# Sixteen experts in a row: gathers over the first seven, scatters from the eighth on

## The chip, the cores and the metric

One Trainium2 chip, one of its cores. The time is device microseconds of one launch. The kernel before takes 2141.14 us (median of three runs, 2135.18 to 2143.14); the execution that was profiled took 2138.47 us.

## The reference, cut to what matters

One layer of a diffusion backbone over 512 latent tokens of 1024 channels. A token mixer comes first; the change lies wholly in the mixture of experts behind it. Each of 16 experts takes the 64 tokens that have the highest affinity for it, and all matrices are fp32:

```python
def ec_moe(h, router, w1, w3, w2):
    b_, n, _ = h.shape
    cap = EC_CAPACITY * n // N_EXPERTS          # 64
    aff = jax.nn.softmax(jnp.einsum('bld,de->ble', h, router).astype(F32), axis=-1)
    gate, idx = lax.top_k(jnp.swapaxes(aff, 1, 2), cap)
    xe = h[bidx, idx]
    hid = jax.nn.silu(jnp.einsum('becd,edf->becf', xe, w1)) * jnp.einsum('becd,edf->becf', xe, w3)
    ye = jnp.einsum('becf,efd->becd', hid, w2) * gate[..., None].astype(h.dtype)
    return jnp.zeros_like(h).at[bidx, idx].add(ye)
```

w1, w3 and w2 of an expert are 1024 x 1024 each, 12 MiB together; all 192 MiB are read once.

## The kernel before, in words

**Experts.** `experts` (L1678) runs over e = 0 to 15. An expert has four parts on TensorE. `front` (L1701) makes the two input products, `ph`, from its 64 gathered tokens `xe` and the eight pieces of w1 and w3; a piece is 1 MiB. In the **gap** behind it ScalarE copies `ph` out, `hidden` (L1769) transposes it (`pht`) and ScalarE and VectorE make silu times the second product, in two halves. `gates` (L1781) makes the gate of each slot (`pgt`), from experts 4 to 14 also `by_slot` (L1762), the transposed one-hot rows by slot (`poh`, kept in `O[e]`). `back` (L1791) makes the output product `pye` from four pieces of w2, a `yield` after each, and scales it into `yf[e]`. `split` (L1809) cuts `yf[e]` into a high and a low part, `Y[e]`.

**Gathers and scatters.** `gather(h)` (L1657) makes `xe` for experts 4h to 4h+3 as products of the tokens (`xH`, `xL`) with one-hot matrices `OH`; it has eight units, each 8 matmuls `rp` and one ScalarE copy. `scatter` (L1817) adds the results of a pair of experts to the 512 rows of `acc` (`psc` on TensorE, `macc` on VectorE), in eight units. `acc` and `ys` (which holds `O` and `Y`) lie in the memory of `xH` and `xL`, so no scatter can come before the last gather. Where the loop hands a generator to `front` as `fill`, its units stand between the input products; where it hands it to `more`, they stand in the gap: two ahead of each half of `hidden` and the rest behind (`GB`, L54).

**What sets the order.** Inside the experts TensorE's order is the order of the code (`ME`, L64); the other engines' is set by a scheduler. The number of gather units in the gap of expert e is `GU[e]` (L53). The 24 units of gathers 1 to 3 stand at experts 1, 2 and 3; scatters of pairs (0,1), (2,3), (4,5) in the gaps of experts 4, 5, 6; those of (6,7) to (12,13) as `fill` in the fronts of experts 8, 10, 12 and 14.

**The weight stream.** SyncE issues the weight pieces in order (`w_load`, L1587). Eighteen are asked for before the stage; from then on 13 buffers (`slots`) go round, so a piece is issued when TensorE has used the piece that its buffer held.

Of the kernel before, what the change touches and what calls it, by code (L numbers as in the profile page):

```python
# [8 lines left out]
F32 = mybir.dt.float32  # L9
# [9 lines left out]
D = 1024  # L19
# [30 lines left out]
WA = 8  # L50
SP = 1
CP = 0
GU = 0, 6, 9, 9  # L53
GB = 2, 2, 2  # L54
WC = 0
WB = 50
# [30 lines left out]
class Block:  # L87
# [1569 lines left out]
    def gather(self, ps, tags, h):  # L1657

        nc = self.nc
        xH, xL = self.xHL  # L1660
        if h < 3:
            x = (self.rp if h == 2 else self.op).tile([128, 1 + h // 2, KT, 4, 64], F32, name="xe", tag="B" if h == 2 else f"xe{h}")
            self.xe += [x[:, j] for j in range(1 + h // 2)]
        oh = self.op.tile([128, 4, 4, 64], F32R, name="OH", tag="OH", bufs=1)
        n = 4 if h else 1
        for i in range(0, 4, n):
            self.one_hot(oh[:, i:i + n], self.posT[:, i:i + n, 4 * h:4 * h + 4])
        for kt in range(KT):
            pt = ps.tile([128, 256], F32, name="rp", tag=tags[kt % len(tags)], bufs=2)
            for i in range(4):  # L1670
                o = oh[:, i].rearrange("p e s -> p (e s)")
                nc.tensor.matmul(pt, xH[:, i, kt * 128:kt * 128 + 128], o, start=i == 0, stop=False)
                nc.tensor.matmul(pt, xL[:, i, kt * 128:kt * 128 + 128], o, start=False, stop=i == 3)
            nc.scalar.activation(self.xe[h][:, kt].rearrange("p e s -> p (e s)"), pt, AF.Identity,
                                 bias=self.mod2[:, 1, kt:kt + 1], scale=self.mod2[:, 0, kt:kt + 1])
            yield

    def experts(self, slots, hl, rp, pool, ps):  # L1678
# [76 lines left out]
        def twice(e):  # L1755

            if e not in OH:
                o2 = OH[e] = self.op.tile([128, 4, 2, 64], F32R, name="o2", tag="o2", bufs=1)
                self.one_hot(o2, self.posT[:, :, e:e + 1].to_broadcast([128, 4, 2]))
            return OH.pop(e).rearrange("p i a s -> p i (a s)")  # L1760

        def by_slot(e, o2):  # L1762
            po = ps.tile([128, 512], F32, name="poh", tag="pt", bufs=2)
            for i in range(4):
                nc.tensor.transpose(po[:, i * 128:i * 128 + 128], o2[:, i].bitcast(F32), self.ident)
            O[e] = self.ys[:, 4 + e % 4]
            nc.scalar.activation(O[e], po, AF.Copy)
# [13 lines left out]
        def gates(e):  # L1781

            o2 = twice(e)
            pg = ps.tile([128, 2], F32, name="pgt", tag="pt", bufs=2)
            for i in range(4):
                nc.tensor.matmul(pg, o2[:, i], self.affr[:, i, e], start=i == 0, stop=i == 3)
            nc.vector.reduce_sum(self.gate[:, e:e + 1], pg, axis=AX.X)
            if 3 < e < 15:
                by_slot(e, o2)

        def back(e):  # L1791

            py = ps.tile([128, 512], F32, name="pye", tag="py", bufs=2)
            for k in range(4):
                w2 = take(12 * e + 8 + k)
                for j in range(2):
                    kt = 2 * k + j
                    for c in range(2):
                        nc.tensor.matmul(py[64 * c:64 * c + 64], hd[e][:, kt], w2[j][:, 512 * c:512 * c + 512],  # L1799
                                         start=kt == 0, stop=kt == 7, skip_group_check=True)  # L1800
                yield
            if e == 15:
                return py
            yf[e] = yfs.rearrange("p a (b f) -> p (a b) f", b=2)[:, e % 4]
            nc.scalar.activation(yf[e], py, AF.Copy, scale=self.gate[:, e:e + 1])
            if e > 6:
                split(e)

        def split(e):  # L1809

            Y[e] = [self.ys[:, 2 * (e % 2) + h] for h in range(2)]
            for h, y in enumerate(Y[e]):
                own, other = slice(64 * h, 64 * h + 64), slice(64 - 64 * h, 128 - 64 * h)
                nc.scalar.activation(y[own], yf[e][own], AF.Copy)  # L1814
                nc.vector.tensor_sub(y[other], yf[e][own], y[own].bitcast(F32))  # L1815

        def scatter(grp):  # L1817
            for i in range(4):
                for h in range(2):
                    pc = ps.tile([128, 512], F32, name="psc", tag="psc", bufs=2)  # L1820
                    for k, e in enumerate(grp):
                        nc.tensor.matmul(pc, O[e][:, i * 128:i * 128 + 128], Y[e][h], start=k == 0, stop=k == len(grp) - 1)  # L1822
                    a = self.acc[:, i, 512 * h:512 * h + 512]
                    if grp[0] == 0:
                        nc.vector.tensor_copy(a, pc)
                    else:
                        nc.vector.tensor_add(a, a, pc)  # L1827
                    yield
# [50 lines left out]
                nc.sync.dma_start(self.out[0, i * 128:i * 128 + 128, :], self.acc[:, i])  # L1879
        if SP:  # L1880
            self.tc.keep_in_program_order(nc.scalar.activation(self.gate[:, 0:1], self.eps, AF.Sigmoid))
        rest = itertools.chain(*(self.gather(ps, ["psc"], h) for h in (1, 2, 3)))
        for e in range(16):
            g, fill, steps = iter(()), iter(()), 8 * (1,)

            more = itertools.islice(rest, GU[e]) if e < 4 else iter(())
            if e == 0:
                g = self.gather(ps, ["pt", "psc"], 0)
                next(g)
            elif e in (4, 5, 6):  # L1890
                if e == 6:
                    split(5)
                more = scatter([2 * e - 8, 2 * e - 7])
            elif 7 < e < 15 and e % 2 == 0:
                fill = scatter([e - 2, e - 1])
            elif e == 13:

                fin = self.op.tile([128, 4, 512], F32, name="fin", tag="xe0")
                fin2 = self.op.tile([128, 4, 512], F32, name="fin", tag="xe1")
                idx = fin2[:, 1, 176:177].bitcast(I32)  # L1900
                G = fin2[:, 2:4].rearrange("p a f -> p (a f)")
                nc.gpsimd.dma_start(G, self.Gd[1:2, :].to_broadcast([128, D]))
                Gh, pairs, row, half = fin[:, 0], fin2[:, 1, 0:128], fin2[:, 1, 128:132], fin2[:, 1, 132:133]
                for h in range(2):
                    nc.gpsimd.dma_start(Gh[64 * h:64 * h + 64], self.Gd[1:2, 512 * h:512 * h + 512].to_broadcast([64, 512]))
                for h in range(2):
                    nc.vector.tensor_add(pairs[:, 64 * h:64 * h + 64], self.ident[:, 0:64], self.ident[:, 64:128])
                nc.gpsimd.iota(row, pattern=[[256, 4]], base=0, channel_multiplier=2, allow_small_or_imprecise_dtypes=True)
                nc.vector.memset(half, 0.0)
                nc.vector.memset(half[64:128], 1.0)  # L1910
                nc.gpsimd.tensor_scalar(G, G, -.5, None, op0=OP.mult)
                nc.gpsimd.tensor_scalar(Gh, Gh, -.5, None, op0=OP.mult)
                o2 = twice(15)
                fill = itertools.chain(places(o2), tokens(fin[:, 1], self.x1, o2))
            elif e == 15:
                o2 = twice(15)
                OH[15] = o2.rearrange("p i (a s) -> p i a s", a=2)
                sc, tk = scatter([14]), tokens(fin[:, 2], self.acc, o2)
                fill = (next(sc if x == "s" else tk, None) for x in FO)
                with self.tc.manual_schedule(engines=set(ML)):  # L1920
                    py = front_last(fill, ST)
                break
            front(e, g, fill, steps)
            for f in range(3):
                for _ in range(GB[f]):
                    next(more, None)
                if f < 2:
                    hidden(e, f)
            self.finish(more)
            if e == 3:  # L1930
                self.finish(rest)
                self.acc = hl.tile([128, 4, D], F32, name="macc", tag="hlH")
                self.ys = hl.tile([128, 8, 512], F32R, name="yhl", tag="hlL")
            for n in {3: (0, 1), 4: (2, 3)}.get(e, ()):
                by_slot(n, twice(n))
            for n in {3: (0, 1), 4: (2, 3), 5: (4,), 7: (6,)}.get(e, ()):
                split(n)
            gates(e)
            self.finish(back(e))

        (x, a, y), g = (fin[:, i] for i in (1, 2, 3)), fin2[:, 0]
        ss, rs = fin2[:, 1, 133:134], fin2[:, 1, 134:135]
# [173 lines left out]
```

## Time and profile before

| | |
|---|---|
| median of three runs | 2141.14 us |
| profiled execution | 2138.47 us |
| span of its trace | 2136.7 us |
| TensorE busy | 1880.0 us (88%) |
| VectorE busy | 1244.5 us (58%) |
| ScalarE busy | 840.0 us (39%) |
| mean granted TensorE clock | 0.933 |

The page also cuts the span into 40 slices of 53.4 us. TensorE's digits are 9 through the experts' stage up to its end (slices 31 to 39), and a busy digit does not tell products that pace the kernel from products that could have come earlier. The line under it, gigabytes a second, stands at 292, 355, 333 and 362 in slices 31 to 34 and at 409 in slices 35 to 39. Read the two together: where the bytes run at one steady top rate, the stream sets the pace; where they fall below it, something holds the stream back.

### The profile page before, as it was taken

To read this page: it belongs to the slowest core of one execution; us is meant where nothing else is said; L and a number is where in the kernel's file an instruction comes from. 1 tells how busy PE (TensorE), PEld (TensorE's weight loads), DVE (VectorE), ACT (ScalarE), POOL (GpSimd) and SP (SyncE) were. 2 spreads that over 40 slices of the span, in tenths; PEclk is the share of its full clock that TensorE was granted. 3 is DMA by queue.
4 is the path that set the end of the run, shared out by engine and by line. 5 is a ranking of instruction groups with operands and counts; after the bars stand their busy time and mean duration, and the time that the engine had idled before them with its cause. 6 is when DMAs were issued, how large, how long until landed. Compare 5 with 4: busy or idle time off the path is not lost.

```text
span 2136.7 us, 34532 instructions
## 1 busy us (share of the span) xinstructions
PE 1880.0 (88%) x13683; PEld 1255.7 (59%) x13696; DVE 1244.5 (58%) x2234; ACT 840.0 (39%) x1344; POOL 259.2 (12%) x383
## 2 busy tenths in 40 slices
PE   5978898888869988999998997799999999999997
PEld 2867676676646756667675664377877453433332
DVE  4466988897888567555654898864364022322224
ACT  5454565545624343443543453353233131111113
POOL 1123323133220000000000000000001000000002
PEclk8999989999979989999998998889999999999998
DMA  6357687777888766785536353358567989999997
GB/s 239 89 128 179 161 201 181 177 175 184 206 199 241 229 225 217 257 254 157 180 102 203 121 170 104 108 180 287 187 247 292 355 333 362 409 409 409 409 409 292
DMA packets 388414, 495.13 MB, mean 232 GB/s; under 512 B 138521, under 2 KB 278031, under 8 KB 385179
## 3 DMA queue, kind: packets, MB, share of 16 engines
q1 hardware_dynamic: 349883, 407.33, 57.4%
q0 software_dynamic: 21504, 68.70, 11.0%
q10 hardware_dynamic: 16864, 16.88, 2.5%
q8 instruction: 108, 1.77, 0.3%
q14 instruction: 55, 0.45, 0.1%
HBM read 393.96 MB, written 97.98 MB: 230 GB/s over the span
## 4 chain that ended last, share of the span: by engine, by line
PE 53%; DVE 18%; DMA 13%; ACT 8%; issue 6%; POOL 1%; SPq 1%; ACTq 0%; POOLq 0%; DVEq 0%
PE ph L1712 9%; PE pl L311 9%; DMA wraw<-in_w_in_dram 5%; PE pye L1799 5%; PE pch L901 4%; PE mp L1361 4%; PE pc L314 3%; DVE wlo L286 2%; DMA ew<-in_exp_w_dram 2%; PE psc L1822 1%; PE sps L1180 1%; ACT whi L283 1%; PE py L901 1%; PE pl L1314 1%; PE adaps L167 1%
## 5 line engine op out<-in xcount | busy, mean ns | idle before, releaser
L311 PE MATMUL pl<-hlH,whi 128*128 128x512 f32 x672 | 244.1, 443 | 14.2 <-ACT u L455 5.6
L311 PE MATMUL pl<-hlH,wlo 128*128 128x512 f32 x672 | 236.3, 428 | 0.0
L311 PE MATMUL pl<-hlL,whi 128*128 128x512 f32 x672 | 231.9, 425 | 0.0
L1713 PE MATMUL ph<-ew,xe 128*64 128x512 f32 x432 | 196.3, 597 | 2.1 <-DMA ew<-in_exp_w_dram 2.1
L1712 PE MATMUL ph<-ew,xe 128*64 128x512 f32 x432 | 196.0, 596 | 0.0
L283 ACT ACTIVATE whi<-wraw 128x1024 fp32r<-128x1024 f32 x93 | 97.8, 1052 | 182.2 <-DMA wraw<-in_w_in_dram 79.1
L311 PEld LDWEIGHTS pl<-hlH,whi 128*128 128x128 f32 x672 | 132.8, 202 | 56.7 <-issue 14.1
L286 DVE TENSOR_TENSOR wlo<-wraw,whi 128x1024 fp32r<-128x1024 f32 x93 | 112.8, 1212 | 84.1 <-ACT whi L283 58.7
L311 PEld LDWEIGHTS pl<-hlL,whi 128*128 128x128 f32 x672 | 129.3, 196 | 38.1 <-issue 11.4
L311 PEld LDWEIGHTS pl<-hlH,wlo 128*128 128x128 f32 x672 | 128.3, 196 | 36.6 <-issue 12.6
L1712 PEld LDWEIGHTS ph<-ew,xe 128*64 128x64 f32 x432 | 56.3, 137 | 105.9 <-issue 104.5
L1799 PE MATMUL pye<-ew,ewx 128*64 128x512 f32 x448 | 108.3, 635 | 0.0
L314 PE MATMUL pc<-hcH,whi 128*128 128x256 f32 (+1 forms) x312 | 97.2, 315 | 7.1 <-ACT u L455 6.1
L464 DVE SCALAR_TENSOR_TENSOR cacc<-u,cst,cacc 128x772 f32<-128x772 f32 (+1 forms) x96 | 93.3, 972 | 11.1 <-ACT cacc L460 9.6
L314 PE MATMUL pc<-hcL,whi 128*128 128x256 f32 (+1 forms) x312 | 94.6, 307 | 0.0
L314 PE MATMUL pc<-hcH,wlo 128*128 128x256 f32 (+1 forms) x312 | 94.4, 304 | 0.0
L1719 ACT ACTIVATE ewx<-ph 128x512 f32<-128x512 f32 x30 | 17.9, 598 | 187.2 <-PE ph L1713 170.0
L1827 DVE TENSOR_TENSOR macc<-macc,psc 128x512 f32<-128x512 f32 x56 | 37.7, 685 | 91.4 <-PE psc L1822 91.3
L314 PEld LDWEIGHTS pc<-hcH,whi 128*128 128x128 f32 (+1 forms) x312 | 63.0, 202 | 15.8 <-ACT u L455 9.2
L1799 PEld LDWEIGHTS pye<-ew,ewx 128*64 128x64 f32 x448 | 32.7, 146 | 63.8 <-issue 63.1
L1815 DVE TENSOR_TENSOR yhl<-yf,yhl 64x512 fp32r<-64x512 f32 x30 | 20.5, 686 | 81.0 <-ACT yhl L1814 80.5
L1217 ACT ACTIVATE X<-selb,ncumT 128x128 f32<-128x128 f32 x128 | 36.4, 367 | 78.4 <-PE selb L1214 78.3
(594 smaller groups left out, 4100.4 us busy)
## 6 DMA issues: line engine op xcount, KB each, us to landing
ew<-in_exp_w_dram SPq DMA_DIRECT2D x126, 1024.0 KB
ew<-in_exp_w_dram SPq DMA_DIRECT2D x90, 512.0 KB
wraw<-in_w_in_dram SPq DMA_DIRECT2D x83, 512.0 KB
adaw<-in_ada_w_dram SPq DMA_DIRECT2D x24, 1024.0 KB
cst<-in_exp_w_dram SPq DMA_DIRECT2D x14, 1024.0 KB
BTd<-BT ACTq DMA_DIRECT2D x48, 256.0 KB
sAL<-ALd SPq DMA_DIRECT2D x23, 512.0 KB
sBT<-BTd SPq DMA_DIRECT2D x23, 512.0 KB
```

The lines of the kernel that those rows point to most:

```text
L283: pin(nc.scalar.activation(hi, raw, AF.Copy))
L286: self.lo.tensor_sub(lo, raw, hi.bitcast(F32))
L311: nc.tensor.matmul(pl[:n], w_[:, kt, :n], x[0][:, kt, :], **e)
L314: nc.tensor.matmul(pc[:n], w_[:, kt, :n], x[1][:, kt, :], **e)
L464: e.scalar_tensor_tensor(acc[:, s0:s0 + n0], u[:, s0 + k:s0 + k + n0], cw[:, b, k:k + 1], acc[:, s0:s0 + n0], op0=OP.mult, op1=OP.add)
L901: mm = lambda o, w, x, f=True, l=True: nc.tensor.matmul(o, w, x, start=f, stop=l, skip_group_check=True)
L1217: nc.scalar.activation(X[:, c], pt[d][:, c], AF.Identity, bias=self.ncumT[:, c, r:r + 1])
L1361: nc.tensor.matmul(po[ob], w[k][lo][:, ob * 128:ob * 128 + 128], yb[k][:, h], start=k + h + lo == 0, stop=k == 15 and lo == 1)
L1712: nc.tensor.matmul(ph[e][f][0:64], x, w1[j][:, fs], start=kt == 0, stop=kt == 7, skip_group_check=True)
L1713: nc.tensor.matmul(ph[e][f][64:128], x, w3[j][:, fs], start=kt == 0, stop=kt == 7, skip_group_check=True)
L1799: nc.tensor.matmul(py[64 * c:64 * c + 64], hd[e][:, kt], w2[j][:, 512 * c:512 * c + 512], start=kt == 0, stop=kt == 7, skip_group_check=True)
L1827: nc.vector.tensor_add(a, a, pc)
```

## The change: what it does

The gather units are spread: 3, 3, 2, 6, 5, 5 in the gaps of experts 1 to 6. `xe` of gather 2 takes the memory of gather 0, and gather 3 goes into a tile of the memory that held two early weight pieces and gathers 2 and 3 before. As `acc` and `ys` now come after expert 6, the outputs of experts 0 to 7 wait in `yf` (those of 4 to 7 in the other half of that tile). The seven pairs are scattered in the gaps of experts 7 to 12 and 14, none in a front. The rows by slot of experts 0 to 9 are made from a new one-hot during the output products of the expert ahead of the scatter: one after two pieces, one after all four.

On ScalarE, expert 2 of the kernel before, from its copies of `ph` (`ewx<-ph`) to its result (`yf`); `xe<-rp` is a gather unit, `ewx<-pht` a half of the activation:

```order
L1719 ACTIVATE ewx<-ph 128x512 x2
L1674 ACTIVATE xe<-rp,mod_7996 128x256 x2
L1777 ACTIVATE ewx<-pht 128x256
L1674 ACTIVATE xe<-rp,mod_7996 128x256 x2
L1777 ACTIVATE ewx<-pht 128x256
L1674 ACTIVATE xe<-rp,mod_7996 128x256 x5
L1805 ACTIVATE yf<-pye,gate 128x512
```

The same expert in the changed kernel:

```order
L1720 ACTIVATE ewx<-ph 128x512 x2
L1675 ACTIVATE xe<-rp,mod_7996 128x256 x2
L1778 ACTIVATE ewx<-pht 128x256
L1675 ACTIVATE xe<-rp,mod_7996 128x256
L1778 ACTIVATE ewx<-pht 128x256
L1806 ACTIVATE yf<-pye,gate 128x512
```

Nine units have become three; the five that followed the second half are gone.

On TensorE, the gap and output products of expert 8 of the kernel before, whose front holds a scatter (its last unit is the first row):

```order
L1822 MATMUL psc<-yhl 128x512 x2
L1775 MATMUL pht<-ident,ewx 128x128 x8
L1786 MATMUL pgt<-rt_14982,o_16454 128x2 x4
L1765 MATMUL poh<-ident,o_16454 128x128 x4
L1799 MATMUL pye<-ew,ewx 64x512 x16
```

The same stretch of the changed kernel:

```order
L1823 MATMUL psc<-yhl 128x512 x4
L1776 MATMUL pht<-ident,ewx 128x128 x4
L1823 MATMUL psc<-yhl 128x512 x4
L1776 MATMUL pht<-ident,ewx 128x128 x4
L1823 MATMUL psc<-yhl 128x512 x8
L1787 MATMUL pgt<-rt_14982,o_16351 128x2 x4
L1800 MATMUL pye<-ew,ewx 64x512 x8
L1766 MATMUL poh<-ident,o_16359 128x128 x4
L1800 MATMUL pye<-ew,ewx 64x512 x8
L1766 MATMUL poh<-ident,o_16384 128x128 x4
```

The whole scatter has moved into the gap, and two groups of rows by slot, of experts 4 and 5, cut the output products.

```diff
@@ -50,7 +50,7 @@
 WA = 8
 SP = 1
 CP = 0
-GU = 0, 6, 9, 9
+GU = 0, 3, 3, 2, 6, 5, 5
 GB = 2, 2, 2
 WC = 0
 WB = 50
@@ -1659,8 +1659,9 @@
         nc = self.nc
         xH, xL = self.xHL
         if h < 3:
-            x = (self.rp if h == 2 else self.op).tile([128, 1 + h // 2, KT, 4, 64], F32, name="xe", tag="B" if h == 2 else f"xe{h}")
-            self.xe += [x[:, j] for j in range(1 + h // 2)]
+            self.xe.append(self.op.tile([128, KT, 4, 64], F32, name="xe", tag=f"xe{h % 2}"))
+        else:
+            self.xe.append(self.later[:, 1].rearrange("p a (k e s) -> p (a k) e s", e=4, s=64))
         oh = self.op.tile([128, 4, 4, 64], F32R, name="OH", tag="OH", bufs=1)
         n = 4 if h else 1
         for i in range(0, 4, n):
@@ -1785,7 +1786,7 @@
             for i in range(4):
                 nc.tensor.matmul(pg, o2[:, i], self.affr[:, i, e], start=i == 0, stop=i == 3)
             nc.vector.reduce_sum(self.gate[:, e:e + 1], pg, axis=AX.X)
-            if 3 < e < 15:
+            if 9 < e < 15:
                 by_slot(e, o2)
 
         def back(e):
@@ -1801,9 +1802,9 @@
                 yield
             if e == 15:
                 return py
-            yf[e] = yfs.rearrange("p a (b f) -> p (a b) f", b=2)[:, e % 4]
+            yf[e] = (self.later[:, 0] if 3 < e < 8 else yfs).rearrange("p a (b f) -> p (a b) f", b=2)[:, e % 4]
             nc.scalar.activation(yf[e], py, AF.Copy, scale=self.gate[:, e:e + 1])
-            if e > 6:
+            if e == 14:
                 split(e)
 
         def split(e):
@@ -1879,21 +1880,20 @@
                 nc.sync.dma_start(self.out[0, i * 128:i * 128 + 128, :], self.acc[:, i])
         if SP:
             self.tc.keep_in_program_order(nc.scalar.activation(self.gate[:, 0:1], self.eps, AF.Sigmoid))
+        SC = {7: (0, 1), 8: (2, 3), 9: (4, 5), 10: (6, 7), 11: (8, 9), 12: (10, 11), 14: (12, 13)}
         rest = itertools.chain(*(self.gather(ps, ["psc"], h) for h in (1, 2, 3)))
         for e in range(16):
             g, fill, steps = iter(()), iter(()), 8 * (1,)
 
-            more = itertools.islice(rest, GU[e]) if e < 4 else iter(())
+            more = itertools.islice(rest, GU[e]) if e < 7 else iter(())
             if e == 0:
                 g = self.gather(ps, ["pt", "psc"], 0)
                 next(g)
-            elif e in (4, 5, 6):
-                if e == 6:
-                    split(5)
-                more = scatter([2 * e - 8, 2 * e - 7])
-            elif 7 < e < 15 and e % 2 == 0:
-                fill = scatter([e - 2, e - 1])
-            elif e == 13:
+            elif e == 4:
+                self.later = self.rp.tile([128, 2, 2, D], F32, name="ewB2", tag="B")
+            elif e in SC:
+                more = scatter(SC[e])
+            if e == 13:
 
                 fin = self.op.tile([128, 4, 512], F32, name="fin", tag="xe0")
                 fin2 = self.op.tile([128, 4, 512], F32, name="fin", tag="xe1")
@@ -1912,7 +1912,7 @@
                 nc.gpsimd.tensor_scalar(Gh, Gh, -.5, None, op0=OP.mult)
                 o2 = twice(15)
                 fill = itertools.chain(places(o2), tokens(fin[:, 1], self.x1, o2))
-            elif e == 15:
+            if e == 15:
                 o2 = twice(15)
                 OH[15] = o2.rearrange("p i (a s) -> p i a s", a=2)
                 sc, tk = scatter([14]), tokens(fin[:, 2], self.acc, o2)
@@ -1927,16 +1927,23 @@
                 if f < 2:
                     hidden(e, f)
             self.finish(more)
-            if e == 3:
+            if e == 6:
                 self.finish(rest)
                 self.acc = hl.tile([128, 4, D], F32, name="macc", tag="hlH")
                 self.ys = hl.tile([128, 8, 512], F32R, name="yhl", tag="hlL")
-            for n in {3: (0, 1), 4: (2, 3)}.get(e, ()):
-                by_slot(n, twice(n))
-            for n in {3: (0, 1), 4: (2, 3), 5: (4,), 7: (6,)}.get(e, ()):
-                split(n)
             gates(e)
-            self.finish(back(e))
+            outputs = back(e)
+            for n in SC.get(e + 1, ()):
+                if n < 10:
+                    o2 = twice(n)
+                    next(outputs)
+                    next(outputs)
+                    by_slot(n, o2)
+                if n < e:
+                    split(n)
+            self.finish(outputs)
+            if e in SC.get(e + 1, ()):
+                split(e)
 
         (x, a, y), g = (fin[:, i] for i in (1, 2, 3)), fin2[:, 0]
         ss, rs = fin2[:, 1, 133:134], fin2[:, 1, 134:135]
```

## Rows read from the trace of the kernel before

**Rows 1.** Windows of the experts' stage: length, busy time, granted clock, DMA share, GB/s
```profile
core 0: us, PE busy (x) PEld busy (x) DVE busy (x) ACT busy (x) POOL busy (x), PEclk, DMA share, GB/s
1640.00:1660.00 20.00, 19.18 (x106) 9.71 (x106) 2.81 (x6) 4.74 (x9) 0.00 (x0) 1.00 0.81 300
1660.00:1680.00 20.00, 20.00 (x96) 6.48 (x92) 0.67 (x2) 1.20 (x2) 0.00 (x0) 1.00 0.84 316
1680.00:1700.00 20.00, 20.00 (x122) 11.50 (x122) 2.44 (x6) 5.32 (x11) 0.00 (x0) 1.00 0.93 360
1700.00:1720.00 20.00, 19.03 (x126) 12.82 (x124) 3.43 (x7) 6.83 (x13) 0.00 (x0) 1.00 1.02 409
1720.00:1740.00 20.00, 20.00 (x94) 6.46 (x90) 0.14 (x1) 1.28 (x2) 0.00 (x0) 1.00 0.92 353
1740.00:1760.00 20.00, 15.93 (x104) 12.58 (x104) 7.89 (x13) 9.72 (x18) 2.60 (x3) 0.88 0.79 294
1760.00:1780.00 20.00, 20.00 (x89) 6.35 (x86) 0.00 (x0) 1.34 (x3) 0.00 (x0) 0.95 0.96 359
1780.00:1800.00 20.00, 15.90 (x66) 8.22 (x67) 11.28 (x20) 5.40 (x10) 0.00 (x0) 0.83 0.79 307
1800.00:2080.00 280.00, 268.17 (x1194) 100.34 (x1192) 67.21 (x127) 43.16 (x77) 3.52 (x3) 0.99 1.03 409
```
**Rows 2.** Timeline, TensorE: first product of experts 2, 3, 4 and 5
```profile
1694.21 0.59 PE L1712 MATMUL ph<-cst,xe 128*64 128x512 f32 x1
1726.20 0.59 PE L1712 MATMUL ph<-ew,xe 128*64 128x512 f32 x1
1765.91 0.59 PE L1712 MATMUL ph<-ew,xe 128*64 128x512 f32 x1
1801.52 0.59 PE L1712 MATMUL ph<-ew,xe 128*64 128x512 f32 x1
```
**Rows 3.** Timeline, TensorE: expert 5 from its gap to expert 6
```profile
1815.35 1.19 PE L1822 MATMUL psc<-yhl 128*128 128x512 f32 x4
1821.90 0.66 PE L1765 MATMUL poh<-ident,o 128*128 128x128 f32 x4
1822.48 7.09 PE L1799 MATMUL pye<-ew,ewx 128*64 128x512 f32 x32
1829.40 0.59 PE L1712 MATMUL ph<-ew,xe 128*64 128x512 f32 x1
```
**Rows 4.** Timeline, TensorE: gap of expert 1
```profile
1680.14 0.38 PE L1672 MATMUL rp<-OH,xH 128*128 128x256 f32 x1
1682.16 0.60 PE L1775 MATMUL pht<-ident,ewx 128*128 128x128 f32 x4
1686.86 0.50 PE L1786 MATMUL pgt<-rt,o 128*128 128x2 f32 x4
```
**Rows 5.** Timeline, SyncE: issues of weight pieces round expert 3's gap
```profile
1740.12 0.88 SPq L1595 DMA_DIRECT2D ew<-in_exp_w_dram  x2
1759.83 4.05 SPq L1595 DMA_DIRECT2D ew<-in_exp_w_dram  x4
```
**Rows 6.** Timeline, TensorE: waits in experts 2, 3, 4, and expert 3's output products
```profile
1711.63 0.36 PE L1672 MATMUL rp<-OH,xH 128*128 128x256 f32 x1 [0.97 <-DVE OH L1655]
1755.16 1.01 PE L1786 MATMUL pgt<-rt,o 128*128 128x2 f32 x4 [1.87 <-ACT yhl L1767]
1756.11 9.97 PE L1799 MATMUL pye<-ew,ewx 128*64 128x512 f32 x32
1789.16 1.07 PE L1765 MATMUL poh<-ident,o 128*128 128x128 f32 x4 [2.64 <-DVE o L1655]
```
**Rows 7.** One line's instructions: the one-hot rows, durations min/median/max
```profile
L1655 DVE TENSOR_TENSOR o<-rt x21: 679/692/694, 1633.5 to 2085.5; 128x512 fp32r<-128x512 f32 x21
```
**Rows 8.** Timeline, TensorE: its last wait for a weight piece
```profile
2061.54 0.64 PE L1713 MATMUL ph<-ew,xe 128*64 128x512 f32 x1 [0.34 <-DMA ew<-in_exp_w_dram]
```
**Rows 9.** Windows: where the weight stream ends
```profile
2116.00:2120.00 4.00, 4.00 (x21) 1.29 (x17) 3.93 (x5) 2.28 (x4) 4.00 (x4) 1.00 0.82 329
```

## The prediction, before the run

> **What bounds the kernel now.** I looked first at the page's row of gigabytes a second by slice, because the experts do one fixed thing: read 192 MiB once. From 1800 to 2080 us the windows show 409 GB/s with the DMA engines' share at 1.03 [rows 1]: no more fits. One piece of 1 MiB (1.0486 MB) then takes 1.0486/0.409 = 2.56 us, and an expert's twelve 30.8 us. That is the pace of the second half, whatever TensorE does.
>
> Next I asked what held the stream below 409 before 1800. The same windows give 300, 316, 360, 409, 353, 294, 359 and 307 from 1640 on [rows 1]. The starts of the experts on TensorE say why: expert 2 takes 1726.20 - 1694.21 = 32.0 us, expert 3 39.7, expert 4 35.6 [rows 2], all longer than 30.8, while expert 5 takes 1829.40 - 1801.52 = 27.9 [rows 2, 3]. The 13 buffers are full, and a piece can be asked for only when an old one has been used. SyncE's own rows show it: nothing is issued between 1740.12 and 1759.83 [rows 5], while TensorE stands in expert 3's gap and begins its output products at 1756.11 [rows 6]. So early on TensorE paces the stream, later the stream paces itself, and bytes not moved early can't be caught up later at a rate that is already full.
>
> The third view is the end. TensorE's last wait for a piece is at 2061.54 [rows 8], and the rate falls off in the window from 2116 [rows 9]; I take 2117 for the last piece. From 2061.54 on TensorE runs through its own work, a few us behind the stream.
>
> **The change part by part.** Prices first. The front without insertions takes 1815.35 - 1801.52 = 13.8 us [rows 2, 3]. From the front's end to the next expert it is 1829.40 - 1815.35 = 14.05 with a scatter in the gap [rows 3], and 1694.21 - 1680.14 = 14.07 with six gather units [rows 2, 4]: the two fillings cost the same, 27.9 us for the expert. Two gather units and the switch behind them take 1682.16 - 1680.14 = 2.0 us [rows 4], so I price a unit at 1.0. One group of rows by slot takes 1822.48 - 1821.90 = 0.6 us [rows 3].
>
> With these, TensorE's need in the changed kernel:
> - Experts 1 and 2, three units each: 27.9 - 3 x 1.0 = 24.9. Expert 3, two units: 23.9. Where a gap becomes short, a wait for the activation comes back, under 1 us of it.
> - Expert 4, six units: 27.9. Expert 5, five units, with the turn from gather 2 to 3 inside the gap: 26.9 plus the 0.97 that this turn cost in expert 2 [rows 6] = 27.9.
> - Expert 6, five units and two groups of rows: 26.9 + 1.2 = 28.1.
> - Experts 7 to 9, a scatter, two groups of other experts' rows, none of its own: 27.9 + 1.2 - 0.6 = 28.5. Expert 10, all three groups: 29.1. Experts 11, 12 and 14: 27.9, as expert 5.
> - Expert 13 keeps its fill.
>
> Every one is below the stream's 30.8. Experts 2 to 5 together need 24.9 + 23.9 + 27.9 + 27.9 = 104.6 us instead of 1829.40 - 1694.21 = 135.2. But those 30.6 us are not the gain: TensorE may go no further ahead than the pieces. The gain is what the stream had lost. Its shortfall against 409 from 1680 to 1800 is 49 + 0 + 56 + 115 + 50 + 102 = 372 GB/s, in windows of 20 us [rows 1]: 7.44 MB, or 18.2 us at 409. The shortfall of 1640 to 1680, 109 + 93 = 202, belongs to expert 0, which is unchanged, and to the first buffers; that stays. Of the 49 in 1680 to 1700, the gap of expert 1, I leave 20 standing, since a shorter gap is still a gap: 1.0 us. So the last piece lands 17.2 us sooner, about 2100.
>
> Does the end follow it? Before, TensorE ended its products behind the last piece, and expert 15 is unchanged. Expert 14 gets shorter on TensorE, but the last quarter of its front must still wait for its pieces, and gap, output products and expert 15 follow as one dense chain. So I take the same distance: end earlier by 17.2. What appears in its place are waits of TensorE for pieces, some 30.8 - 28.5 = 2.3 us an expert from about expert 6 on.
>
> What I cost at nothing. The gather and scatter instructions are the same in number. Six more one-hots are built, 0.69 us each on VectorE [rows 7], 4 us in all; the first stands behind the gate's reduction while TensorE has half of its output products to do (7.09/2 = 3.5 us [rows 3]), the second has the other half. If that cover fails, TensorE stands at the transposes; the price is in the second rival. The scatter leaves the fronts of experts 8, 10, 12 and 14; that frees TensorE, which then waits longer for pieces: nothing. Results of experts 4 to 7 go into the tile of two early pieces; those are used up in expert 1. SyncE's list of pieces is in the same order. On GpSimd two loads of the last scale now wait for expert 11's front and stand behind the other load; what is queued behind them is wanted only in expert 15.
>
> A rule of the Trainium skill speaks against the full sum. Its page "DMA: Bandwidth & Descriptors", section "Where 436 GB/s comes from", says that for HBM to SBUF the HBM side binds at about 358 GB/s per core. Counted against 358, only 353, 294 and 307 fall short, by 120 GB/s over 20 us, an estimate of 6.7 us of gain. The trace disagrees, with 409 over 280 us [rows 1], on a core that runs alone; the measurement decides.
>
> Sum: 2138.47 - 18.2 + 1.0 = 2121.3 us. The profiled execution lies 2.7 us below the median 2141.14. I forecast 2121, with 2115 to 2127 as its own range: the price of a gather unit hardly matters, since there are 2 to 6 us of room per expert, and what remains is how much of expert 1's loss returns, and the distance at the end.
>
> **The rivals.**
>
> The stream is freed wholly. If the pieces of experts 0 and 1 also came at 409, the shortfall of 1640 to 1800 would all return: 574 GB/s x 20 us / 409 = 28.1 us, 2110. For it: expert 1 uses its pieces sooner. Against: expert 0 is the same, and some of the first buffers are used once only. This is a floor, since TensorE's own 30.6 us and the shorter later fronts can't outrun the pieces.
>
> The rows by slot stall. In experts 3 and 4, where the kernel before built rows for other experts, TensorE stood 1.87 us for a ScalarE copy and 2.64 for a one-hot [rows 6]. If each of experts 6 to 10 pays both, 28.5 + 4.5 = 33.0 against 30.8, it loses 2.2 x 5 = 11 us: 2132. For: the same instructions on the same three engines, and the splits stand between. Against: the stalls came where two groups and the splits stood back to back; now 3.5 us of products lie between.
>
> The clock, the slow side. Waits are exactly what this change adds to TensorE. In expert 3, behind its waits, the output products took 9.97 us [rows 6] where 7.09 is the full price [rows 3], 2.9 more, and the granted clock of the window round their start is 0.88, of 1780 to 1800 0.83 [rows 1], a mixture of the levels 1.2 and 2.4 GHz. If each of experts 6 to 14 paid 2.9 twice, once behind a wait for pieces in the front and once behind the gap, it would need 28.5 + 5.8 = 34.3, 3.5 over the stream, 31 us in nine experts: 2138.5 - 17.2 + 31 = 2152. It decides from 28.5 + x > 30.8 + 17.2/9, that is x = 4.2 us lost per expert. The Trainium skill's "TensorE: Matmul & The Clock Gate", section "HAM oscillation — how this bites in real kernels", tells of this chain: a wait for DMA in every tile, and each next tile starts cold. Against: the trace's waits for pieces are short (0.34 us [rows 8]), a slow stretch only shortens the next wait, since the stream runs on, and from 1800 to 2080 the clock was 0.99 [rows 1] with gaps in every expert.
>
> The change doesn't free the stream. If the pauses of SyncE came from the queue itself, the rate would stay as it is: 2138. Against: the pause ends 3.7 us after the output products of expert 3 begin, when the first of their pieces is used [rows 5, 6].
>
> **How the numbers follow.** Forecast 0.70, stream wholly freed 0.09, stalls at the rows 0.09, clock 0.06, not freed 0.06. A difference under 0.5%, 10.7 us, can't be told from no change. Faster: 0.70 + 0.09 = 0.79. Same: stalls and not freed, 0.15. Slower: clock, 0.06. The range, 2110 to 2133, goes from the floor to the stalls and leaves out the last two, 0.12.
>
> **What would show it.** Right: 400 GB/s and more in every window from 1700 to the end; experts 1 to 3 at 24 to 26 us each on TensorE; waits of TensorE for `ew` in most experts from 6 or 7 on, 15 to 25 us in all; no pause of SyncE as long as the one at 1740; experts 7 to 14 at about 30.8 us. Wrong: windows under 380 between 1700 and 1800 (a gap still holds the stream); waits for one-hots or copies at the transposes of experts 6 to 10; a granted clock under 0.9 from expert 6 on with experts longer than 31 us; or the last piece at 2100 and the end no nearer to it.

## The result: 0.8% faster, by what the stream had lost

The changed kernel takes 2122.66 us (median of 5 runs, 2119.16 to 2128.71), the kernel before 2139.74 beside it (5 runs): ratio 0.9921, interval 0.9897 to 0.9946. The forecast was 2121, the range 2110 to 2133. The profiled execution took 2122.66 us, its span is 2120.9.

The instructions ahead of expert 0 are the same in both kernels, yet expert 0 began anywhere from 1635 to 1648 us in the profiled runs of this study. So I also measure the **stage**, from expert 0's first `ph` to the end of the last `pye`: two executions of the changed kernel, with starts 5 us apart, gave 471.71 and 471.60. First and last row of it on TensorE in the kernel before (start us, duration us):

```profile
1635.09 0.64 PE L1712 MATMUL ph<-ew,xe 128*64 128x512 f32 x1
...
2120.44 3.65 PE L1799 MATMUL pye<-ew,ewx 128*64 128x512 f32 x16
```

The changed kernel, with the starts of experts 2 to 6 on the way:

```profile
1636.56 0.64 PE L1713 MATMUL ph<-ew,xe 128*64 128x512 f32 x1
...
1693.14 0.59 PE L1713 MATMUL ph<-cst,xe 128*64 128x512 f32 x1
...
1718.51 0.59 PE L1713 MATMUL ph<-ew,xe 128*64 128x512 f32 x1
...
1744.13 0.59 PE L1713 MATMUL ph<-ew,xe 128*64 128x512 f32 x1
...
1772.03 0.59 PE L1713 MATMUL ph<-ew,xe 128*64 128x512 f32 x1
...
1800.17 0.59 PE L1713 MATMUL ph<-ew,xe 128*64 128x512 f32 x1
...
2104.62 3.65 PE L1800 MATMUL pye<-ew,ewx 128*64 128x512 f32 x16
```

The stage was 2124.09 - 1635.09 = 489.00 and is 2108.27 - 1636.56 = 471.71 us: 17.3 shorter. The span shows 15.8 of it, since expert 0 began 1.5 us later. Experts 2, 3 and 4 take 25.4, 25.6 and 27.9 us, where they took 32.0, 39.7 and 35.6 [rows 2].

The windows of the changed kernel, in the columns of [rows 1]:

```profile
1640.00:1660.00 20.00, 19.53 (x104) 9.18 (x100) 1.86 (x3) 4.60 (x9) 0.00 (x0) 1.00 0.82 305
1660.00:1680.00 20.00, 19.65 (x94) 7.04 (x96) 1.62 (x5) 1.07 (x2) 0.00 (x0) 1.00 0.81 309
1680.00:1700.00 20.00, 19.89 (x108) 9.22 (x106) 2.26 (x6) 4.13 (x8) 0.00 (x0) 1.00 1.02 406
1700.00:1720.00 20.00, 19.89 (x110) 9.37 (x108) 2.26 (x6) 4.13 (x8) 0.00 (x0) 1.00 1.03 410
...
1780.00:1800.00 20.00, 19.03 (x112) 10.28 (x110) 3.56 (x7) 4.58 (x9) 0.00 (x0) 1.00 1.03 409
1800.00:2064.00 264.00, 249.26 (x1146) 100.27 (x1142) 75.75 (x140) 50.21 (x91) 6.12 (x6) 1.00 1.03 408
...
2100.00:2104.00 4.00, 4.00 (x20) 1.19 (x16) 3.93 (x5) 2.26 (x3) 4.00 (x4) 1.00 0.81 327
```

Read the last column downward: from 1680 to 2064 us the stream stands at 406 to 410 GB/s, where it was 294 to 409 up to 1800; in the first two windows it is what it was. It falls off in the window from 2100, before in that from 2116 [rows 9]. SyncE, which paused from 1740.12 to 1759.83 [rows 5], now issues without such a pause. The 15 issues from 1725.57 on are 12 pieces, since three of the 13 buffers are filled in two halves; the last row ends where the view was cut:

```profile
1725.57 29.38 SPq L1595 DMA_DIRECT2D ew<-in_exp_w_dram  x15
1755.84 0.37 SPq L1595 DMA_DIRECT2D cst<-in_exp_w_dram  x1
1757.12 14.94 SPq L1595 DMA_DIRECT2D ew<-in_exp_w_dram  x7
```

What TensorE waits for in the changed kernel (us in all, times, longest): on its matmul rows from 1630 to 2121,

```profile
PE ph L1714 <- DMA ew<-in_exp_w_dram: 9.5, 13, 1.5
PE pgt L1787 <- DVE ewx L1780: 2.7, 3, 1.3
...
PE ph L1714 <- DMA cst<-in_exp_w_dram: 1.5, 1, 1.5
```

and on its weight loads, `PEld`, from 1800 to 2070 (the first column of numbers is again the sum):

```profile
PEld ph L1714 <- DMA ew<-in_exp_w_dram: 23.6, 18, 2.3
```

Both say that TensorE now waits for pieces. The sizes differ, since the matmul rows count idle time only from the modelled end of the products still in flight.

### The profile page after: what moved, and what is told of

The parts are those of the page before. It is cut to its first block, busy times and chain, and to the rows that moved or that the text cites. A ratio compares the mean times of both kernels' runs of the same rounds, so it can differ in the third digit from the quotient of the medians.

```text
span 2120.9 us, 34560 instructions
## 1 busy us (share of the span) xinstructions
PE 1865.1 (88%) x13683; PEld 1251.7 (59%) x13696; DVE 1245.5 (59%) x2240; ACT 838.0 (40%) x1344; POOL 256.3 (12%) x383
## 3 DMA queue, kind: packets, MB, share of 16 engines
q0 software_dynamic: 21504, 68.70, 11.1%
## 4 chain that ended last, share of the span: by engine, by line
PE 50%; DVE 18%; DMA 17%; ACT 7%; issue 6%; SPq 1%; POOL 1%; ACTq 0%; POOLq 0%; DVEq 0%
PE pl L311 9%; PE ph L1713 6%; DMA ew<-in_exp_w_dram 5%; DMA wraw<-in_w_in_dram 5%; PE pch L901 4%; PE pye L1800 4%; PE mp L1361 4%; PE pc L314 3%; DVE wlo L286 2%; PE pl L1314 2%; PE sps L1180 1%; PE py L901 1%; DMA BTd<-BT 1%; PE adaps L167 1%; PE ph L1714 1%
## 5 line engine op out<-in xcount | busy, mean ns | idle before, releaser
L1714 PE MATMUL ph<-ew,xe 128*64 128x512 f32 x336 | 148.8, 594 | 4.4 <-DMA ew<-in_exp_w_dram 4.4
L311 PEld LDWEIGHTS pl<-hlL,whi 128*128 128x128 f32 x672 | 128.5, 195 | 37.9 <-issue 11.4
L1713 PE MATMUL ph<-ew,xe 128*64 128x512 f32 x336 | 148.7, 594 | 0.0
L311 PEld LDWEIGHTS pl<-hlH,wlo 128*128 128x128 f32 x672 | 127.3, 195 | 35.6 <-issue 11.7
L1800 PE MATMUL pye<-ew,ewx 128*64 128x512 f32 x448 | 101.4, 597 | 0.0
L1713 PEld LDWEIGHTS ph<-ew,xe 128*64 128x64 f32 x336 | 44.7, 137 | 78.9 <-issue 76.5
L1779 DVE TENSOR_TENSOR ewx<-ewx,pht 128x256 f32<-128x256 f32 x32 | 13.4, 419 | 108.3 <-ACT ewx L1778 108.0
L314 PEld LDWEIGHTS pc<-hcL,whi 128*128 128x128 f32 (+1 forms) x312 | 60.7, 196 | 4.4 <-issue 2.1
```

The costliest lines, as they stand in the source:

```text
L311: nc.tensor.matmul(pl[:n], w_[:, kt, :n], x[0][:, kt, :], **e)
L314: nc.tensor.matmul(pc[:n], w_[:, kt, :n], x[1][:, kt, :], **e)
L1713: nc.tensor.matmul(ph[e][f][0:64], x, w1[j][:, fs], start=kt == 0, stop=kt == 7, skip_group_check=True)
L1714: nc.tensor.matmul(ph[e][f][64:128], x, w3[j][:, fs], start=kt == 0, stop=kt == 7, skip_group_check=True)
```

## Experiments

Ratios are against the kernel before, run on the same chip with each. The part ahead of the stage varied by up to 13 us, so the stage is what I compare: 489.0 before, 471.7 changed. Differences are taken from 471.6, the second profile of the changed kernel. Each edit is to the changed kernel, unless it says otherwise. My theory is that of the forecast: the stream sets the end, and the change lets it run from expert 1 on.

**The changed kernel again**, beside the others.

> The changed kernel once more, beside the next three on the same chip: 2119 to 2125.

2126.98 us, ratio 0.9921 (0.9904 to 0.9937), stage 471.60. The time is 2 us above what I expected and the kernel before, at 2144.15, was slower beside it too; the ratio is the same as in the result.

**Is it TensorE's work, or the stream?** Two edits take from one and leave the other alone. First, the scatters of experts 8 to 12 left out:

```diff
-                more = scatter(SC[e])
+                more = scatter(SC[e]) if e in (7, 14) else iter(())
```

> The changed kernel without the scatters of experts 8 to 12: the results of pairs (2,3) to (10,11) are left out of the sum, 40 units of TensorE and VectorE, 5 x 3.5 us of TensorE. All weights are read as before. Theory: the stream paces, the waits for pieces grow by 17 us and the time stays within 2 us of the changed kernel. Rival (TensorE paces): 10 to 17 us sooner.

Ratio 0.9909 (0.9890 to 0.9929), stage 471.65: 17.5 us less of TensorE work (40 units, as estimated), 0.0 gained. The weight loads' wait for `ew`, 23.6 us in the changed kernel, grew by 19.3, so what TensorE saves it waits (1800 to 2075):

```profile
PEld ph L1714 <- DMA ew<-in_exp_w_dram: 42.9, 29, 3.0
```

Second, one piece less in four late experts, the piece ahead of it used twice:

```diff
-                w2 = take(12 * e + 8 + k)
+                if k < 3 or e not in (7, 9, 11, 13):
+                    w2 = take(12 * e + 8 + k)
```

> The changed kernel that leaves out four weight pieces: the last w2 piece of experts 7, 9, 11 and 13 isn't loaded, and its products take the third piece's weights again. TensorE's work is the same, the stream is 4 MiB shorter. Measured from expert 0's first product to the last output product, where the changed kernel takes 471.7 us in two profiles. Theory (the stream paces): 4 x 2.56 = 10.2 us sooner, less a little where an expert's need on TensorE (28.5) comes near the stream's new pace: 462 to 465. Rival (TensorE paces): the same 471 to 472.

Ratio 0.9891 (0.9863 to 0.9919), stage 464.25: 7.4 us gone where TensorE's products are all still there, and its matmul rows' wait for `ew` falls from 9.5 to 4.9 us. From about expert 7 on the stream is the bound: the two together show it. The opposite edit, the first piece of experts 7 to 14 loaded twice:

```diff
-                pin(self.nc.sync.dma_start(..., src[:, n * j:n * j + n]))
+                for _ in range(2 if i in range(84, 180, 12) else 1):
+                    pin(self.nc.sync.dma_start(..., src[:, n * j:n * j + n]))
```

> The changed kernel, which loads the first weight piece of experts 7 to 14 twice into the same buffer: 8 MiB more, no other work. Theory: the stream is the bound from 1680 us to its end, every piece costs its full 2.56 us: + 20.5 us, 2143. Rival (TensorE paces, the stream has room): only the waits grow, + 5 us or less.

Ratio 1.0084 (1.0054 to 1.0114), stage 507.45, 35.8 more where 20.5 was expected. The stream's end did move by what eight pieces cost, about 22 us. But TensorE lost more, waiting for pieces up to 18.9 us at once. The first view is its waits; the second is the window of the longest one, with the stream at its full rate:

```profile
PE ph L1714 <- DMA ew<-in_exp_w_dram: 42.6, 5, 18.9
```

```profile
1840.00:1860.00 20.00, 1.51 (x4) 0.53 (x6) 0.31 (x1) 0.21 (x1) 0.00 (x0) 0.55 1.03 410
```

Why a doubled piece holds TensorE that long I did not settle; as a measure of a piece this run is spoilt.

**Which part of the change does it?** The scatters of experts 8, 10, 12 and 14 moved from front to gap in the kernel before, and nothing else:

```diff
-                fill = scatter([e - 2, e - 1])
+                more = scatter([e - 2, e - 1])
```

> The kernel before with one part of the change alone: the scatters of experts 8, 10, 12 and 14 go from the fronts into the gaps. That takes some 3 us of TensorE from each of four experts. Theory: the stream is full from 1800 us on and was already late there; TensorE waits longer for pieces, and the time stays that of the kernel before within 3 us (2136 to 2140; expert 14's gap, on the chain of the end, grows as its front shrinks). Rival: TensorE paces the second half too, and 4 x 3 = 12 us are gained: 2127.

Ratio 1.0004 (0.9989 to 1.0018), stage 489.0, as before. Then, in the changed kernel again, its gather units in two clumps:

```diff
-GU = 0, 3, 3, 2, 6, 5, 5
+GU = 0, 8, 0, 0, 16, 0, 0
```

> The changed kernel with its gather units bunched again: 8 in the gap of expert 1, 16 in that of expert 4, none in 2, 3, 5 and 6 (3, 3, 2, 6, 5, 5 before); scatters, rows by slot and buffers stay. TensorE's work is the same. Theory (the stream lost its time where an expert took longer than its 30.8 us): expert 4 needs 27.9 + 10 = 38 us on TensorE, 7 over the stream's pace; the rate falls under 409 GB/s round expert 4's gap alone, and the end comes 4 to 8 us later than in the changed kernel: 2126 to 2130. Rival (the gain is TensorE's, from gaps that are filled and scatters that left the fronts): the same 24 units in gaps, no difference: 2122.

Ratio 0.9946 (0.9928 to 0.9964), stage 475.92, 4.3 more, as expected in size. The place was not: expert 4, with 16 units and 39.1 us, cost nothing, and the loss stands behind expert 1's eight units (1680 to 1720) and not at 1760:

```profile
1680.00:1700.00 20.00, 20.00 (x130) 12.59 (x128) 3.58 (x7) 6.28 (x12) 0.00 (x0) 1.00 1.00 397
1700.00:1720.00 20.00, 19.18 (x96) 7.06 (x94) 1.54 (x5) 2.55 (x5) 0.00 (x0) 1.00 0.88 340
1720.00:1740.00 20.00, 20.00 (x96) 6.53 (x92) 0.72 (x2) 1.18 (x2) 0.00 (x0) 1.00 1.03 408
1760.00:1780.00 20.00, 18.59 (x142) 15.84 (x139) 2.91 (x5) 9.32 (x18) 0.00 (x0) 1.00 1.03 408
```

The two windows lack 12 + 69 GB/s of 409 over 20 us, 4.0 us of the 4.3. Experts 2 and 3, with empty gaps, took 23.4 us each and used their pieces early, so that expert 4 could be long: not every expert by itself has to stay under 30.8. Nor is the sum of the experts since the start the rule. Experts 0 and 1 took 31.2 + 29.8 = 61.0 us, under 2 x 30.8, and the loss is there, right behind the windows up to 1680 in which the stream stands below its rate in every run.

Next, all seven scatters of the changed kernel in the fronts, with the gaps empty:

```diff
-                more = scatter(SC[e])
+                fill = scatter(SC[e])
```

> The changed kernel with all seven scatters between the input products, as the kernel before had four of them, and no unit in a gap from expert 7 on. Fronts go from 13.9 to 19.9 us of TensorE's own time, gaps from 7 to 3.5; experts 7 to 9 then need 13.9 + 6 + 3 + 8.1 = 31 us, at the stream's 30.8. Theory: waits for pieces give way to scatter units, and the end stays or comes up to 3 us sooner, since expert 14's gap, on the chain of the end, is shorter: 2119 to 2123. Rival (the place of the scatters in the gaps made the gain): 7 x 2.5 = 17 us are lost again, 2139.

Ratio 0.9959 (0.9936 to 0.9981), stage 483.03, 11.4 more: neither theory had it. The stream holds 407 to 410 GB/s from 1680 to 1980 and ends in the window from 2104; read in steps of 0.5 us, its last bytes come at about 2106.5. But TensorE's last product ends at 2123.6, 17 us behind (5 in the changed kernel, read in the same way), since experts 7 to 11 take 32.3 to 34.9 us. Its waits (1825 to 2030) and rows of expert 8's gap, with ScalarE's and VectorE's, show why:

```profile
PE pgt L1787 <- DVE ewx L1780: 11.6, 6, 2.3
```

```profile
1885.77 0.93 PE L1776 MATMUL pht<-ident,ewx 128*128 128x128 f32 x7
1885.92 1.15 ACT L1815 ACTIVATE yhl<-ewB 64x512 fp32r<-64x512 f32 x2
1886.59 1.29 DVE L1816 TENSOR_TENSOR yhl<-ewB,yhl 64x512 fp32r<-64x512 f32 x2
1888.93 0.58 PE L1787 MATMUL pgt<-rt,o 128*128 128x2 f32 x4 [2.24 <-DVE ewx L1780]
1889.44 5.35 PE L1800 MATMUL pye<-ew,ewx 128*64 128x512 f32 x16
```

```profile
1860.00:1880.00 20.00, 20.00 (x86) 6.30 (x82) 4.82 (x7) 1.77 (x3) 2.78 (x1) 1.00 1.03 408
1880.00:1900.00 20.00, 17.76 (x80) 6.91 (x80) 8.01 (x15) 5.84 (x11) 0.00 (x0) 0.91 1.03 409
1920.00:1940.00 20.00, 17.77 (x79) 6.35 (x76) 6.83 (x13) 3.57 (x7) 0.00 (x0) 0.91 1.03 409
2104.00:2108.00 4.00, 4.00 (x20) 1.37 (x20) 1.54 (x4) 2.13 (x7) 0.00 (x0) 1.00 0.33 130
```

This gap waits 2.2 us for the activation, and the sixteen output products behind it take 5.35 us where the full price is 3.65 (the last row of the changed kernel, above). It isn't emptiness alone that costs 2.2: the scheduler had put `split`s (`yhl`, L1815 and L1816) ahead of the activation on both engines. In this run gaps with two splits there (experts 7 to 10) wait 2.2 to 2.3 us, with one (expert 11) 1.6, with none (expert 12) 1.0; the gaps that the run without scatters emptied wait 0.7. And the wait alone doesn't set the 5.35 us: expert 7 waited as long and paid 3.65. Four units in the front and four in the gap:

```diff
                 more = scatter(SC[e])
+                fill = itertools.islice(more, 4)
```

> The changed kernel with each scatter cut in two: four units in the front, where TensorE waits for pieces, four in the gap. Fronts need 13.9 + 4 x 0.75 = 16.9 us, gaps some 5, so an expert 29.7, still under 30.8. Theory (the stream paces, and scatters in all fronts cost 11 us because an expert then took 32 to 35): no loss, and 0 to 2 us sooner by expert 14's shorter gap: stage 469.5 to 472. Rival (every unit in a front costs, since it breaks up the products): half of the 11 us, 477.

Ratio 0.9920 (0.9904 to 0.9937), stage 471.06. So units may stand in the front, as long as some are left for the gap: four were enough. Little room is left, though: the matmul rows' wait for `ew` is down to 0.2 us, and experts 10 and 11 took 35.2 and 32.5 us without a loss in the stage.

The third part: the rows by slot built back to back ahead of the gates, with the splits, as experts 3 and 4 did in the kernel before:

```diff
+            for n in SC.get(e + 1, ()):
+                if n < 10:
+                    by_slot(n, twice(n))
+            for n in SC.get(e + 1, ()):
+                if n < e:
+                    split(n)
             gates(e)
             outputs = back(e)
-            for n in SC.get(e + 1, ()):
-                if n < 10:
-                    o2 = twice(n)
-                    next(outputs)
-                    next(outputs)
-                    by_slot(n, o2)
-                if n < e:
-                    split(n)
```

> The changed kernel with the rows by slot of other experts ahead of the gate, as in experts 3 and 4 of the kernel before, one group straight behind the other, and the splits behind them; experts 6 to 10. Each waits for a one-hot and for copies: 1.9 + 2.6 us where the kernel before showed them. TensorE then needs 28.5 + 4.5 = 33 us against 30.8. Theory: 2.2 us lost in each of experts 6 to 10 at most, less where the waits for pieces only shrink: 2 to 11 us later than the changed kernel. Rival (the place of the rows is nothing): the same time.

Ratio 0.9971 (0.9956 to 0.9987), stage 482.75, 11.1 more. Experts 6 to 10 take 34.6 to 36.1 us; the waits are of the kind of [rows 6] (1825 to 2050), the clock falls behind them, and at last the stream too:

```profile
PE poh L1766 <- DVE o L1655: 12.0, 5, 3.3
PE pgt L1787 <- DVE o L1655: 4.6, 4, 1.5
```

```profile
1920.00:1940.00 20.00, 15.86 (x66) 7.76 (x64) 11.18 (x20) 5.45 (x10) 0.00 (x0) 0.85 1.02 406
1940.00:1960.00 20.00, 20.00 (x92) 6.58 (x89) 0.00 (x0) 1.57 (x3) 0.00 (x0) 0.98 0.96 368
1960.00:1980.00 20.00, 15.95 (x70) 8.15 (x70) 11.28 (x20) 5.17 (x10) 0.00 (x0) 0.83 0.85 328
```

**What is left?** The 305 and 309 GB/s of 1640 to 1680 are worth about 10 us. Are the buffers what holds them? One fewer, 12, and so one piece fewer asked for ahead (`PO` loses its last entry with `PL`):

```diff
-PL = (0, 1, -1, -2, 2, 3, 4, 5, 6, 7)
+PL = (0, 1, -1, -2, 2, 3, 4, 5, 6)
...
-EWB = 7
+EWB = 6
```

> The changed kernel with 12 weight buffers that go round, not 13 (and 17 pieces asked for ahead). Theory (what is still lost from 1640 to 1680 us is lost for want of buffers round expert 0, and later the buffers are not full): one piece later, 2.6 us, up to 6 if a gap of experts 1 to 6 now holds the stream too: stage 474 to 478. Rival (it is lost to expert 0's pace on TensorE): the same 471 to 472.

Ratio 0.9947 (0.9930 to 0.9963), stage 473.03, 1.4 more: between the theories. SyncE's own waits in the changed kernel say more. From 1636 to 1680 they are all for TensorE, 41.1 of 44 us:

```profile
SPq L1595 <- PE ph L1714: 35.8, 10, 7.7
SPq L1595 <- PE pye L1800: 5.3, 2, 4.1
```

From 1740 to 1784, at the full rate, about half is for earlier DMA, and the longest wait for TensorE is 2.0 us:

```profile
SPq L1595 <- DMA ew<-in_exp_w_dram: 14.5, 11, 2.2
```

So in these two windows the pieces wait for buffers that TensorE still uses, most of the time for expert 0. Whether more buffers or a quicker expert 0 would bring the 10 us back no run shows.

At the other end, only expert 14's scatter back in its front:

```diff
-                more = scatter(SC[e])
+                if e == 14:
+                    fill = scatter(SC[e])
+                else:
+                    more = scatter(SC[e])
```

> The changed kernel with one scatter moved, that of expert 14 (pair 12, 13), from its gap into its front. In the changed kernel that front takes 19.3 us instead of 13.9 because it waits for pieces; a scatter fits into the waits. The gap shrinks from 7.1 to 3.6 us and lies on the chain of the end. Theory: 2 to 3.5 us sooner than the changed kernel. Rival (the end hangs on the last piece alone): the same time.

Ratio 0.9916 (0.9900 to 0.9932), stage 470.39, 1.2 less where 2 to 3.5 was expected: expert 14 shrinks from 33.3 to 31.5 us and expert 15 grows from 30.1 to 30.6. The same with `GU = 0, 1, 3, 4, 6, 5, 5`:

> The changed kernel with the two edits that the runs point to: expert 14's scatter in its front (stage 470.4 us in one profile, against 471.7), and gather units 1, 3, 4 in the gaps of experts 1 to 3 in place of 3, 3, 2, since the stream still runs below 409 GB/s up to 1680 us, at expert 1. Theory (the stream paces from expert 0 on): expert 1's gap is up to 2 us shorter, its pieces are used sooner, and the stage becomes 468.5 to 470. Rival (the loss there is one of buffers alone, freed by expert 0): 470.4.

Ratio 0.9906 (0.9889 to 0.9922), stage 470.25; expert 1 took 24.4 us and 0.1 came of it, no more than the stage's own spread. This is the shortest stage of those that compute the whole reference, 1.4 us under the changed kernel; whole runs can't tell the two apart.

## Why the prediction was right, point by point

- **The sum.** Forecast: 18.2 us of shortfall back, 1.0 left at expert 1, 17.2 in all. Measured on the stage: 17.3. The term for expert 1 was too large (its window came to 406, which is 0.15 us of shortfall, not 1.0), that for 1640 to 1680 was right (unchanged). With 0.15 the sum would have been 18.05, so 0.7 us were lost at a place I did not find, and that 17.2 met 17.3 is in part luck. The last piece, forecast for about 2100, lands in the window from 2100.
- **"Those 30.6 us are not the gain."** Experts 2 to 5 took 1800.17 - 1693.14 = 107.0 us (forecast 104.6, before 135.2), 28 us less, and the stage only 17.3 less. The run without the scatters and the one with fewer pieces show why: what TensorE saves is waited away, what the stream saves comes back in the main (7.4 of 10.2).
- **Prices.** Experts 1 to 3 took 25.4, 25.4 and 25.6 against 24.9, 24.9 and 23.9. The three gaps that wait for the activation (2.7 us) are those of experts 0, 3 and 13. So in experts 1 and 2, with three units, no such wait is back: three units less saved 2.5 us, 0.8 a unit and not 1.0. Expert 3, with two, waits 1.32 us (forecast under 1). Experts 4 and 5: 27.9 and 28.1 against 27.9.
- **The edits costed at nothing.** Leaving the front gained nothing by itself (stage 489.0 in the kernel before with that edit alone). But in the changed kernel the same move undone (all seven scatters into the fronts) loses 11.4 us, and rows taken out from among the output products lose 11.1. Neither edit makes the gain; both keep what an expert needs of TensorE under 30.8 us. Without the first TensorE falls behind a stream that stays full; without the second the stream waits again too (328 GB/s). Made worse one by one, the three parts cost 4.3 (bunched, though not as in the kernel before), 11.4 and 11.1 us, more than the 17.3 together, so they are conditions of each other and no shares.
- **The same distance at the end** held here: from the start of the window in which the stream falls off to the last product it was 2124.09 - 2116 = 8.1 us and is 8.3. It was right with too weak a reason: it holds only while each expert keeps up with its pieces. With the scatters in the fronts TensorE ended some 17 us behind the last bytes, where it is 5 in the changed kernel.
- **Rivals.** Stream wholly freed: no, 1640 to 1680 didn't move. Not freed: no, the rate rose. Rows that stall: not here (0.3 us at the transposes). With the cover taken away the loss was 11.1 us, the 11 that the rival gave, but that it agrees to a tenth is luck. The rival had 33.0 us for each of experts 6 to 10 and lost 2.2 in each. They took 35.3 in the mean, 21 us more together than in the changed kernel, as the clock fell behind the waits as well; experts 11 to 14, at 27.9 to 29.0, made up 10 of it. The clock: the granted clock stood at 1.00 in the windows shown from 1640 to 2064, behind waits for pieces of 1.5 us and less; with the scatters in the fronts or stalled rows it fell to 0.91 and 0.83 and made up part of the loss. It fell to 0.91 in windows of the run without scatters and of the one with four units in front too, and there the stage lost nothing, as the rival's own counter-argument had it.
- **The signs named ahead.** Waits for pieces, forecast 15 to 25 us: 23.6 by the weight loads, 9.5 + 1.5 by the matmul rows. Experts 7 to 13, forecast at about 30.8 us each, took 29.0 to 32.0, and 30.8 in the mean; expert 14 took 33.3. The sign of 400 GB/s to the end was drawn too wide: from 2064 to 2100 the rate is 392 to 393, as it was 391 from 2080 to 2100 before.
- The Trainium skill's 358 GB/s ("DMA: Bandwidth & Descriptors", "Where 436 GB/s comes from") did not bind: 408 over 264 us here too, and the gain was 17.3, not the 6.7 estimated from it. The same section gives 358 as half of a stack's 716, for two cores, beside a measured 425; the forecast took it for the limit of a core that runs alone.

## What to carry to other kernels

Where weights stream through a ring of buffers, find first the rate that the stream reaches when nothing holds it, and value a change by the bytes that it brings forward, not by the engine time that it saves. Let short consumers stand ahead of a long one: 39.1 us cost nothing behind two of 23.4, while 29.8 us cost 4 where the stream had just been below its rate. Spread the fillers over the gaps between dependent engines, and look at what else the other engines do ahead of the result that a gap waits for. Test the parts of such a change by undoing them one by one: a part can be worth nothing alone and most of the gain when it is missing.

## What was not expected of the hardware

The same instructions ahead of the stage took up to 13 us more or less from one profiled run to another, while the stage repeated to 0.1 us: a mark inside the trace told apart what the whole time could not. And the length of a wait alone did not tell when the granted clock would fall. Thirteen waits for DMA of up to 1.5 us left it at 1.00. With the scatters in the fronts, expert 7's gap waited 2.26 us and the products behind it kept their full price, while expert 8's, with 2.24, came with 0.91 and 5.35 us:

```profile
1856.67 0.58 PE L1787 MATMUL pgt<-rt,o 128*128 128x2 f32 x4 [2.26 <-DVE ewx L1780]
1857.17 3.65 PE L1800 MATMUL pye<-ew,ewx 128*64 128x512 f32 x16
```

In the run without scatters the same 5.35 us stand behind waits of 0.72 and 0.34:

```profile
2009.79 0.58 PE L1787 MATMUL pgt<-rt,o 128*128 128x2 f32 x4 [0.72 <-DVE ewx L1780]
2010.70 0.66 PE L1766 MATMUL poh<-ident,o 128*128 128x128 f32 x4 [0.34 <-DVE gate L1788]
2011.29 5.35 PE L1800 MATMUL pye<-ew,ewx 128*64 128x512 f32 x16
```

What decides between them these runs don't show.
